# Hybrid decoder trunk with eight experts: three places of 96 slots, five lasting weight tiles, and five loads sent in halves

## The chip, the cores and the metric

The kernel runs on one core of a Trainium2 chip; the other seven cores do nothing. The metric is the device time of one execution in microseconds (us), here the median of three runs. The times of single instructions come from one further execution, which the hardware profiler recorded.

## The reference, cut to what matters

256 tokens of 1024 features pass through two layers and a last norm. Layer 0 (two kinds of attention, then a dense SwiGLU) and the attention of layer 1 are not touched by the change. What counts is the last block of layer 1, in which each token goes to the two experts with the highest router logits:

```python
def swiglu(x, w_gate, w_up, w_down):
    return (jax.nn.silu(x @ w_gate) * (x @ w_up)) @ w_down

def moe_swiglu(x, w_router, w_gate, w_up, w_down):      # x: 256 tokens x 1024
    logits = (xt @ w_router).astype(jnp.float32)        # 8 experts
    top_vals, top_idx = lax.top_k(logits, TOP_K)        # TOP_K = 2, ties to the lower index
    top_w = jax.nn.softmax(top_vals, axis=-1)
    gates = jnp.einsum('nk,nke->ne', top_w, jax.nn.one_hot(top_idx, N_EXPERTS, ...))
    for e in range(N_EXPERTS):                          # w_gate[e], w_up[e]: 1024 x 3584, w_down[e]: 3584 x 1024, float32
        y = y + gates[:, e:e + 1] * swiglu(xt, w_gate[e], w_up[e], w_down[e])
```

The 512 choices (256 tokens, two each) are all that has to be computed; the weights of all eight experts have to be read once, whoever uses them.

## The kernel before, in words

**Places and slots.** The experts are run in eight places, one after the other. Place 0 is always expert 0. Which of the experts 1 to 7 stands in places 1 to 7 is settled at run time: `choose` (L929) counts the tokens of each expert on VectorE (DVE), `arrange` (L959) ranks experts 1 to 7 by their count, and place i takes the expert whose rank is `RANKS[i-1]`. Place i has `CAPS[i]` slots, 64 or 96, and every matmul of the place is laid out for that many rows, filled or not. Where an expert has more tokens than its place has slots, `t.over` is positive and the branch at L1317 runs the surplus in a further pass (`rest`), which reads that expert's weights a second time.

**Loads.** The weights of one expert come in 12 loads of 3,584 KB: four of `w_gate`, four of `w_up`, four of `w_down`. That is 96 loads, numbered 1 to 96 here in the order in which they are sent. They go through five buffers in turn (buffer of load n is reused by load n+5), on the DMA queue of the sync engine (SP), which issues in program order: an issue that has to wait holds up all behind it. Loads 1 and 2 are brought in small pieces during layer 0 (`weights.piece`). `experts_open` (L1020) sends loads 3, 4 and 5 into the pool `big2`, which takes memory that layer 1 has just used. From then on `weights.send()` stands behind the matmuls that read a load: when load n has been read, load n+5 is sent into its buffer. The last load of `w_down`, load 96, is sent as three smaller ones.

**The matmuls of a place.** `into` (L1140) multiplies the gathered tokens with a gate or up load into PSUM, in two halves r of the 3,584 columns; `down` (L1186) does it with a `w_down` load. A place of 64 needs two groups of 32 rows, a place of 96 three, and the third group costs its own matmuls: 12 instead of 8 for each row block of a load in `into`, and in `down` those to `yo` (L1197). The order within a place is: two gate loads, two `w_down` loads of the place before, two up loads, two gate loads, two `w_down` loads of this place, two up loads. Between them stand the transposes of the hidden values (L1177), the gathers of the next group of places (L1101) and the scatter of the last place into the residual stream (L1224, L1225). TensorE (PE) runs this order as written.

**Before the experts.** The last projection of layer 1 (`w_out1`) is worked in four parts v0, v1, v2, v3 of 24 matmuls each, in that order, and each part reads one pair of split weight tiles (`whi`, `wlo`), which lie in the memory of three pools `parts0` to `parts2`. Router transposes and logits stand between the matmuls of v3 and behind them.

Of the kernel before, what the change touches and what calls it, by code (L numbers as in the profile page):

```python
# [31 lines left out]

CAPS = (64, 96, 64, 96, 96, 64, 96, 64)
RANKS = (0, 4, 1, 2, 5, 3, 6)

# [54 lines left out]
def trunk(ctx: ExitStack, tc: tile.TileContext, a: dict, out: bass.AP):  # L90
# [41 lines left out]

    turn = [0]

    def raw():
        n = sum(c for _, c, _ in raw_pools)
        i = turn[0] % n
        turn[0] += 1
        for pool, c, size in raw_pools:
            if i < c:  # L140
                break
            i -= c
        return pool.tile([128, size], F32, name="big")

# [172 lines left out]
    onesb = consts.tile([128, 128], BF, name="onesb")  # L317
    lower = consts.tile([128, NE, NE], F32, name="lower")
    place = consts.tile([128, 2, NE], F32, name="place")
    wr = consts.tile([128, KD, NE], F32, name="wr")  # L320
# [24 lines left out]
    def masks():  # L345
        V.tensor_scalar(tri, jp, 0.0, None, op0=OP.is_ge)
        V.tensor_scalar(mcaus[:, 0:128], jp[:, :128], 0.0, NEG, op0=OP.is_gt, op1=OP.mult)
        V.memset(mcaus[:, 128:256], 0.0)
        V.tensor_copy(mcaus[:, 256:384], mcaus[:, 0:128])
        V.tensor_copy(mswa[:, 0:128], mcaus[:, 0:128])  # L350
        V.tensor_scalar(mswa[:, 128:256], jp[:, :128], 0.0, NEG, op0=OP.is_le, op1=OP.mult)
        V.tensor_copy(mswa[:, 256:384], mcaus[:, 0:128])
        G.iota(slot, pattern=[[1, 128]], base=0, channel_multiplier=0, allow_small_or_imprecise_dtypes=True)
        V.tensor_scalar(strict, jp[:, :128], 0.0, None, op0=OP.is_gt)
        V.memset(onesb, 1.0)
        own, other = slot[:, 0:NE, None], slot[:, None, 0:NE]
# [570 lines left out]


    def choose():  # L929
        rp = t.rp  # L930
        t.lg = rp.tile([128, NB, NE], F32, name="lg")
        V.tensor_copy(t.lg, t.pl)
        gt = rp.tile([128, NB, NE, NE], BF, name="gt")
        eq = rp.tile([128, NB, NE, NE], BF, name="eq")
        t.rank = rp.tile([128, NB, NE], F32, name="rank")
        mb = rp.tile([128, NB, NE], BF, name="mb")
        other = t.lg[:, :, None, :].to_broadcast([128, NB, NE, NE])
        own = t.lg[:, :, :, None].to_broadcast([128, NB, NE, NE])
        V.tensor_tensor(eq, other, own, op=OP.is_equal)
        V.tensor_tensor(gt, other, own, op=OP.is_gt)  # L940
        V.tensor_tensor(eq, eq, lower[:, None, :, :].to_broadcast([128, NB, NE, NE]), op=OP.mult)
        V.tensor_tensor(gt, gt, eq, op=OP.add)
        V.tensor_reduce(t.rank, gt, axis=AX.X, op=OP.add)
        V.tensor_scalar(mb, t.rank, 2.0, None, op0=OP.is_lt)
        pp = bank(32)
        T.matmul(pp[:, 0:8], strict, mb[:, 0], start=True, stop=True)
        T.matmul(pp[:, 8:16], onesb, mb[:, 0], start=True, stop=False)
# [3 lines left out]
        far = rp.tile([128, NB, NE], F32, name="far")  # L951
        V.tensor_scalar(far, mb, -1000.0, 1000.0, op0=OP.mult, op1=OP.add)
        t.pos = rp.tile([128, NB, NE], F32, name="pos")
        V.tensor_tensor(t.pos, far, pp[:, 0:16].rearrange("p (b e) -> p b e", b=NB), op=OP.add)
        t.count = rp.tile([128, NE], F32, name="count")
        V.tensor_copy(t.count, pp[:, 16:24])


    def arrange():  # L959
        rp, n = t.rp, NE - 1  # L960
        sq = [128, n, n]
        c = t.count[:, 1:]
        more, same = rp.tile(sq, F32, name="more"), rp.tile(sq, F32, name="same")
        own, other = c[:, :, None].to_broadcast(sq), c[:, None, :].to_broadcast(sq)
# [3 lines left out]
        V.tensor_tensor(more, more, same, op=OP.add)  # L968
        rk = rp.tile([128, n], F32, name="rk")
        V.tensor_reduce(rk, more, axis=AX.X, op=OP.add)  # L970
        t.at = rp.tile(sq, F32, name="at")
        V.tensor_tensor(t.at, rk[:, None, :].to_broadcast(sq), place[:, 1, 1:, None].to_broadcast(sq), op=OP.is_equal)
# [11 lines left out]
    def moved(o, x):  # L984
        n = NE - 1
        p = t.rp.tile([128, n, n], F32, name="moved", bufs=2)
        V.tensor_tensor(p, t.at, x[:, None, 1:].to_broadcast([128, n, n]), op=OP.mult)
# [9 lines left out]
    def gates():  # L997
        rp = t.rp
        t.gate = gate = rp.tile([128, NB, NE], F32, name="gate")
        tw = rp.tile([128, 4, NB], F32, name="tw")  # L1000
        oh = [rp.tile([128, NB, NE], F32, name=f"oh{i}") for i in range(2)]
        mx = [rp.tile([128, NB], F32, name=f"mx{i}") for i in range(2)]
        for i in range(2):
# [9 lines left out]
        V.tensor_tensor(tw[:, 3], tw[:, 1], tw[:, 2], op=OP.mult)  # L1013
        gt2 = rp.tile([128, NB, NE], F32, name="gt2")
        V.tensor_tensor(gate, oh[0], bc(tw[:, 2]), op=OP.mult)
# [4 lines left out]
    def experts_open():  # L1020
# [7 lines left out]
        t.yo = py.tile([128, 256], F32, name="yo")  # L1028
        raw_pools.append((lpool("big2", 3), 3, BIG))
        turn[0] = 2  # L1030
# [23 lines left out]
    class Weights:  # L1054
# [29 lines left out]
    def experts(base, caps, groups, first=(), then=(), finish=()):  # L1084
# [45 lines left out]
        def part_out(e, g, j0, n):  # L1130
            def start(v):
                nc.sync.dma_start(v[:, :n * D], weight("down", e)[g * RG:(g + 1) * RG]
                                  .rearrange("(p j) w -> p (j w)", j=7)[:, j0 * D:(j0 + n) * D])
            return weights.add(start)
# [5 lines left out]
        def into(e, u, k0, key):  # L1140
# [155 lines left out]
    def final3(b):  # L1296
# [4 lines left out]
    finish = [do(final_in)] + [do(final2, b) for b in range(NB)] + [do(final3, b) for b in range(NB)]  # L1301
    mine = experts((0,) * NE, CAPS, ((0,), (1, 2), (3,), (4, 5), (6, 7)), [do(experts_open)],
                   [do(order.close), do(in_order, 'PE'), do(arrange), do(gates), do(read_counts)], finish)
# [52 lines left out]
```

## Time and profile before

| | us |
|---|---|
| median of three runs | 1336.55 (1336.16 to 1337.74) |
| the profiled execution, its own time | 1339.13 |
| its span, first to last instruction | 1337.3 |
| PE busy | 1285.7 (96%) |
| DVE busy | 373.7 (28%) |
| weights and other bytes moved by SP's queue | 428.48 MB, 80.0% of 16 engines' span |

The part with the experts begins near 504 us, when PE reads load 1, and takes the rest of the span. The busy share of PE counts every moment in which a matmul is somewhere in the array, so 96% doesn't yet say that PE decides the time. The other number to keep in view is the rate at which the DMA engines bring weights, stretch by stretch, and how long a load takes from its issue to its landing.

### The profile page before, as it was taken

The numbers are of one execution on the slowest core, as the hardware profiler recorded it, in microseconds if no ns is written. First come the engines' busy times: TensorE is split into PE (matmuls) and PEld (weight loads), VectorE is DVE, ScalarE is ACT, GpSimd is POOL, SyncE is SP. The second block draws the span as 40 slices with busy tenths as digits, with TensorE's granted clock in tenths as the row PEclk, the third lists the DMA queues.
The fourth block names the chain that finished last, engine by engine and source line by source line (L and its number), as shares of the span: only waits on it lengthen the run. The fifth ranks groups of instructions, "written<-read, shape, count | busy, mean of one in ns | idle before, by whom it ended". The sixth has DMA issues, their size and how long they took to land.

```text
span 1337.3 us, 23873 instructions
## 1 busy us (share of the span) xinstructions
PE 1285.7 (96%) x10713; PEld 697.2 (52%) x10713; DVE 373.7 (28%) x697; ACT 303.3 (23%) x495; POOL 167.3 (13%) x116
## 2 busy tenths in 40 slices
PE   7999899999999999999999898999999999999995
PEld 6876678888879783433333332433333343333332
DVE  7666445445465831001012001000201200100202
ACT  6565444443344621100000100100000010000001
POOL 3311344334434110000000000000000000000000
PEclk9999899999999999999999999999999999999997
DMA  8620785555555249999999999999999999999993
GB/s 272 207 93 1 294 287 189 182 177 178 187 166 181 95 183 433 415 427 431 422 426 430 416 428 425 424 432 386 397 384 399 429 420 428 434 419 426 427 426 134
DMA packets 75758, 431.71 MB, mean 323 GB/s; under 512 B 3676, under 2 KB 7792, under 8 KB 71424
## 3 DMA queue, kind: packets, MB, share of 16 engines
q1 hardware_dynamic: 75088, 428.48, 80.0%
q8 instruction: 86, 1.41, 0.4%
q0 software_dynamic: 416, 1.10, 0.2%
q10 hardware_dynamic: 144, 0.52, 0.1%
q14 instruction: 24, 0.20, 0.0%
HBM read 429.04 MB, written 1.05 MB: 322 GB/s over the span
## 4 chain that ended last, share of the span: by engine, by line
PE 82%; DMA 11%; DVE 2%; ACT 1%; POOL 1%; issue 0%; POOLq 0%; ACTq 0%
PE mm L1150 32%; PE y L1193 11%; PE mm L201 8%; PE mm L202 8%; PE mm L203 8%; DMA big<-in_l_w_up_dram 8%; PE yo L1197 4%; DMA big<-in_l_w_down_dram 2%; PE tt L1177 1%; PE tt L1101 1%; PE ww L373 1%; PE ww L203 1%; PE ww L201 1%; PE ww L202 1%; PE mm L416 1%; DMA raw<-in_l_w_gate_dram 1%
## 5 line engine op out<-in xcount | busy, mean ns | idle before, releaser
L1150 PE MATMUL mm<-big,g 128*32 128x448 f32 x5120 | 495.1, 544 | 11.6 <-DMA big<-in_l_w_up_dram 10.5
L1150 PEld LDWEIGHTS mm<-big,g 128*32 128x32 f32 x5120 | 165.4, 111 | 320.1 <-issue 297.5
L1193 PE MATMUL y<-big,ehT 128*32 128x512 f32 x1792 | 215.2, 593 | 0.4 <-DMA big<-in_l_w_down_dram 0.4
L164 POOL TENSOR_TENSOR wlo<-raw,whi 128x288 fp32r<-128x288 f32 (+6 forms) x74 | 154.5, 2089 | 287.2 <-ACT whi L160 266.5
L162 DVE TENSOR_TENSOR wlo<-raw,whi 128x1760 fp32r<-128x1760 f32 (+6 forms) x74 | 143.0, 1934 | 134.0 <-ACT whi L160 133.7
L160 ACT ACTIVATE whi<-raw 128x2048 fp32r<-128x2048 f32 (+4 forms) x74 | 134.4, 1816 | 154.2 <-PE mm L203 82.3
L201 PE MATMUL mm<-whi,xh 128*128 128x512 f32 (+3 forms) x352 | 139.1, 396 | 1.7 <-ACT whi L160 0.9
L202 PE MATMUL mm<-wlo,xh 128*128 128x512 f32 (+3 forms) x352 | 137.2, 390 | 3.0 <-POOL wlo L164 3.0
L203 PE MATMUL mm<-whi,xl 128*128 128x512 f32 (+3 forms) x352 | 137.0, 390 | 1.4 <-DVE xl L290 1.3
L1178 ACT ACTIVATE ehT<-tt 128x512 f32<-128x512 f32 (+1 forms) x32 | 15.6, 487 | 520.3 <-PE tt L1177 520.2
L1164 DVE TENSOR_TENSOR hid<-hid,mm 128x448 f32<-128x448 f32 x40 | 24.9, 621 | 306.8 <-PE mm L1150 303.7
L1294 POOL TENSOR_TENSOR fs<-fs,nhalf 128x1 f32<-128x1 f32 x2 | 1.1, 548 | 830.3 <-DVE fs L1293 830.3
L1193 PEld LDWEIGHTS y<-big,ehT 128*32 128x32 f32 x1792 | 56.9, 110 | 81.5 <-issue 62.9
L201 PEld LDWEIGHTS mm<-whi,xh 128*128 128x128 f32 x352 | 67.7, 192 | 17.6 <-issue 1.8
L202 PEld LDWEIGHTS mm<-wlo,xh 128*128 128x128 f32 x352 | 67.7, 192 | 16.9 <-POOL wlo L164 3.3
L203 PEld LDWEIGHTS mm<-whi,xl 128*128 128x128 f32 x352 | 67.3, 191 | 16.8 <-DVE xl L290 3.1
L1197 PE MATMUL yo<-big,ehT 128*32 128x256 f32 x896 | 68.9, 379 | 0.0
L1197 PEld LDWEIGHTS yo<-big,ehT 128*32 128x32 f32 x896 | 29.1, 110 | 67.0 <-issue 65.3
L201 PE MATMUL mm<-xh,whi 128*128 128x256 f32 x160 | 46.6, 291 | 0.0
L202 PE MATMUL mm<-xl,whi 128*128 128x256 f32 x160 | 45.2, 283 | 0.0
L203 PE MATMUL mm<-xh,wlo 128*128 128x256 f32 x160 | 45.2, 283 | 0.0
L1180 DVE COPY ehT<-tt 128x384 f32<-128x384 f32 x16 | 8.9, 558 | 124.0 <-PE tt L1177 124.0
(310 smaller groups left out, 1048.0 us busy)
## 6 DMA issues: line engine op xcount, KB each, us to landing
big<-in_l_w_up_dram SPq DMA_DIRECT2D x32, 3584.0 KB, 26.8
big<-in_l_w_down_dram SPq DMA_DIRECT2D x31, 3584.0 KB, 26.2
big<-in_l_w_gate_dram SPq DMA_DIRECT2D x30, 3584.0 KB, 24.7
raw<-in_l_w_in_dram SPq DMA_DIRECT2D x15, 1024.0 KB, 5.0
raw<-in_l_w_gate_dram SPq DMA_DIRECT2D x14, 1024.0 KB, 5.0
raw<-in_l_w_up_dram SPq DMA_DIRECT2D x14, 1024.0 KB, 5.0
raw<-in_l_w_down_dram SPq DMA_DIRECT2D x14, 1024.0 KB, 4.9
raw<-in_l_w_out_dram SPq DMA_DIRECT2D x8, 1024.0 KB, 5.0
```

The costliest lines, as they stand in the source:

```text
L160: A.activation(hi, v, AF.Copy)
L162: V.tensor_tensor(lo[:, :, :m], v[:, :, :m], hi[:, :, :m].bitcast(F32), op=OP.subtract)
L164: G.tensor_tensor(lo[:, :, m:], v[:, :, m:], hi[:, :, m:].bitcast(F32), op=OP.subtract)
L201: T.matmul(ps, l[0], r[0], start=first, stop=False, **kw)
L202: T.matmul(ps, l[0], r[1], start=False, stop=False, **kw)
L203: T.matmul(ps, l[1], r[0], start=False, stop=last, **kw)
L373: T.matmul(p[:, i, Q], q[i][:, qs], k[i][:, 0:n], start=True, stop=bias is None)
L1150: T.matmul(ps[key][j][i * O:(i + 1) * O], x[:, k0 + k, g * O:(g + 1) * O], w[:, k, c:c + CH], **at)
L1164: V.tensor_tensor(x[:, g], x[:, g], ps["u"][g], op=OP.mult)
L1178: copy = V.tensor_copy if j0 else lambda a_, b_: A.activation(a_, b_, AF.Copy)
L1193: T.matmul(t.y[c * O:(c + 1) * O], x[:, (2 * i + c % 2) * O:(2 * i + c % 2 + 1) * O], w[:, j, c // 2 * 512:(c // 2 + 1) * 512], **at)
L1197: T.matmul(t.yo[c * O:(c + 1) * O], x[:, (4 + i) * O:(5 + i) * O], w[:, j, c * 256:(c + 1) * 256], **at)
```

## The change

It has five parts. Place 4 goes from 96 slots to 64, so three places of 96 are left (1, 3 and 5) with places of 64 between them; ranks and groups of places are rearranged to fit. The five buffers become five tiles that are allocated once and kept (`buffers`), so that a load waits for the readers of the part that it overwrites and not for the release of a whole tile; `big2` becomes three pools of one tile. Loads 6 to 10 are sent in two parts: the first (`half`) behind the readers of the first half of its buffer, the second where the whole load went before. The many small tiles of the router move from their own pool `rp` into the first 600 or so columns of a tile that is free by then (`tmp` in `t.dr[0]`). And `choose` ranks the logits with three DVE operations (subtract, compare with `least`, sum) instead of five.

```diff
-CAPS = (64, 96, 64, 96, 96, 64, 96, 64)
-RANKS = (0, 4, 1, 2, 5, 3, 6)
+CAPS = (64, 96, 64, 96, 64, 96, 64, 64)
+RANKS = (0, 3, 1, 4, 2, 5, 6)
...
-    turn = [0]
+    turn, buffers = [0], {}
     def raw():
...
-        return pool.tile([128, size], F32, name="big")
+        if at not in buffers:
+            buffers[at] = pool.tile([128, size], F32, name="big")
+        return buffers[at]
...
+        V.tensor_scalar(least, lower, -2.0 ** -126, None, op0=OP.mult)
...
+    def tmp(*shape):
+        n = math.prod(shape)
+        v = t.dr[0][:, t.used:t.used + n]
+        t.used += n
...
-        V.tensor_tensor(eq, other, own, op=OP.is_equal)
-        V.tensor_tensor(gt, other, own, op=OP.is_gt)
-        V.tensor_tensor(eq, eq, lower[:, None, :, :].to_broadcast([128, NB, NE, NE]), op=OP.mult)
-        V.tensor_tensor(gt, gt, eq, op=OP.add)
+        V.tensor_tensor(gt, other, own, op=OP.subtract)
+        V.tensor_tensor(gt, gt, least[:, None, :, :].to_broadcast([128, NB, NE, NE]), op=OP.is_gt)
         V.tensor_reduce(t.rank, gt, axis=AX.X, op=OP.add)
...
-        raw_pools.append((lpool("big2", 3), 3, BIG))
+        raw_pools.extend((lpool(f"big{i}"), 1, BIG) for i in range(2, 5))
...
         def send(self):
             if self.at < len(self.todo):
                 x = self.todo[self.at]
                 self.at += 1
+                if x.tile is not None:
+                    x.start(x.tile, 2, 2)
+                    return
                 x.tile = raw()
                 x.start(x.tile)
+        def half(self):
+            if len(self.todo) > 90 and 5 <= self.at < 10:
+                x = self.todo[self.at]
+                x.tile = raw()
+                x.start(x.tile, 0, 2)
...
         def part_out(e, g, j0, n):
-            def start(v):
-                nc.sync.dma_start(v[:, :n * D], weight("down", e)[g * RG:(g + 1) * RG]
-                                  .rearrange("(p j) w -> p (j w)", j=7)[:, j0 * D:(j0 + n) * D])
+            def start(v, i=0, m=4):
+                a, b = (0, 3, n)[i // 2], (0, 3, n)[(i + m) // 2]
+                nc.sync.dma_start(v[:, a * D:b * D], weight("down", e)[g * RG:(g + 1) * RG]
+                                  .rearrange("(p j) w -> p (j w)", j=7)[:, (j0 + a) * D:(j0 + b) * D])
...
         def into(e, u, k0, key):
...
+                if k == 1:
+                    weights.half()
             weights.send()
...
-    mine = experts((0,) * NE, CAPS, ((0,), (1, 2), (3,), (4, 5), (6, 7)), [do(experts_open)],
+    mine = experts((0,) * NE, CAPS, ((0,), (1, 2), (3, 4), (5, 6), (7,)), [do(experts_open)],
```

Instructions move in two places. The first is SP's queue where the expert loads begin. Before, the third to tenth load (the rows with `big`) stand there so, each with the engines or queues that it waits for; `most` is the table of places that SP reads:

```order
93 L1124 DMA big<-in_l_w_up_dram 128x4x1792 [waits DVE_49,DMASW1_49,PE_49,Activation_49]
94 L1124 DMA big<-in_l_w_up_dram 128x4x1792 [waits DVE_49,PE_49,Pool_49]
95 L1124 DMA big<-in_l_w_gate_dram 128x4x1792
96 L1036 TENSOR_LOAD most [waits DVE_49]
97 L1036 ISA x2
98 L1124 DMA big<-in_l_w_gate_dram 128x4x1792 [waits PE_49]
99 L1132 DMA big<-in_l_w_down_dram 128x7168 [waits PE_49]
100 L1132 DMA big<-in_l_w_down_dram 128x7168 [waits DMAHW4_49,PE_49]
101 L1124 DMA big<-in_l_w_up_dram 128x4x1792 [waits DMAHW5_49,DMAHW2_49,PE_49]
102 L1124 DMA big<-in_l_w_up_dram 128x4x1792 [waits DMAHW6_49,DMAHW3_49,PE_49]
```

In the changed kernel the same stretch of SP's queue reads:

```order
93 L1147 DMA big<-in_l_w_up_dram 128x4x1792 [waits DVE_49,DMASW1_49,PE_49,Activation_49]
94 L1147 DMA big<-in_l_w_up_dram 128x4x1792 [waits PE_49]
95 L1147 DMA big<-in_l_w_gate_dram 128x4x1792 [waits PE_49,Pool_49]
96 L1049 TENSOR_LOAD most [waits DVE_49]
97 L1049 ISA x2
98 L1147 DMA big<-in_l_w_gate_dram 128x2x1792 [waits PE_49] x2
99 L1156 DMA big<-in_l_w_down_dram 128x3072 [waits PE_49]
100 L1156 DMA big<-in_l_w_down_dram 128x4096 [waits DMAHW2_49,PE_49]
101 L1156 DMA big<-in_l_w_down_dram 128x3072 [waits DMAHW4_49,DMAHW3_49,PE_49]
102 L1156 DMA big<-in_l_w_down_dram 128x4096 [waits PE_49]
```

Loads 6 to 10 (row 98 and after) have become two issues each. The waits of loads 4 and 5 (rows 94 and 95) have changed with the memory under them. Before, `rp` ends at byte 111,712 of each partition, the three tiles of `big2` reach up to byte 197,728, and load 4 has the topmost, whose last 1,152 bytes lie in `parts0` (from byte 196,576), where the split weights of v3 are. In the built program load 4 waits for the last matmul of v3, and load 5 stands behind it in the queue and waits for nothing more. In the changed kernel `rp` ends at byte 109,664 and the three tiles end at byte 195,680, below `parts0`. Load 4 now lies over the weights of v1 (in `parts2`) and waits for the last matmul of v1; load 5 lies over those of v2 (in `parts1`) and waits for the last matmul of v2 and for v2's split on POOL.

The second place is PE's order at the change from place 3 to place 4, in r=0 of place 4. Before, both have 96 slots (`mm` is the PSUM tile of gate and up, `hid` the hidden values, `g` the gathered tokens):

```order
2343 L1150 MATMUL mm<-big,g 32x448 x96
2344 L1224 MATMUL tt<-raw,dispT 128x512
2345 L1225 MATMUL tt<-raw,dispT 128x512
...
2352 L1150 MATMUL mm<-big,g 32x448 x48
2353 L1177 MATMUL tt<-ident,hid 128x128 x7
2354 L1150 MATMUL mm<-big,g 32x448 x48
2355 L1177 MATMUL tt<-ident,hid 64x128 x7
```

In the changed kernel place 4 has 64 slots:

```order
2338 L1174 MATMUL mm<-big,g 32x448 x64
2339 L1250 MATMUL tt<-raw,dispT 128x512
2340 L1251 MATMUL tt<-raw,dispT 128x512
...
2347 L1174 MATMUL mm<-big,g 32x448 x32
2348 L1203 MATMUL tt<-ident,hid 128x128 x7
2349 L1174 MATMUL mm<-big,g 32x448 x32
2350 L1124 MATMUL tt<-disp,xg 128x160 x8
```

Each load of place 4 is read by 32 matmuls instead of 48, the second transpose is gone, and the gather of places 5 and 6 stands here.

## Rows read from the trace of the kernel before

**Rows 1.** The page, parts 1 and 2: PE busy, and GB/s in 40 slices.

```profile
PE 1285.7 (96%) x10713; PEld 697.2 (52%) x10713; DVE 373.7 (28%) x697; ACT 303.3 (23%) x495; POOL 167.3 (13%) x116
...
GB/s 272 207 93 1 294 287 189 182 177 178 187 166 181 95 183 433 415 427 431 422 426 430 416 428 425 424 432 386 397 384 399 429 420 428 434 419 426 427 426 134
```

**Rows 2.** The page, part 4: the chain that ended last, by engine.

```profile
PE 82%; DMA 11%; DVE 2%; ACT 1%; POOL 1%; issue 0%; POOLq 0%; ACTq 0%
```

**Rows 3.** Busy time by stretch; last columns: granted clock, DMA share, GB/s.

```profile
530.00:870.00 340.00, 329.86 (x3311) 123.78 (x3307) 32.32 (x62) 28.84 (x66) 0.00 (x0) 0.99 1.01 425
940.00:1050.00 110.00, 109.10 (x1186) 41.43 (x1182) 12.21 (x26) 7.34 (x16) 0.00 (x0) 1.00 0.97 394
```

**Rows 4.** SP's timeline: first issue, time to the end of the last, count.

```profile
469.39 24.78 SPq L1124 DMA_DIRECT2D big<-in_l_w_up_dram  x2
494.22 16.56 SPq L1124 DMA_DIRECT2D big<-in_l_w_gate_dram  x2
...
833.07 12.43 SPq L1124 DMA_DIRECT2D big<-in_l_w_up_dram  x2
...
898.42 9.40 SPq L1124 DMA_DIRECT2D big<-in_l_w_up_dram  x2
...
1015.17 6.40 SPq L1124 DMA_DIRECT2D big<-in_l_w_up_dram  x2
...
1076.73 8.89 SPq L1124 DMA_DIRECT2D big<-in_l_w_gate_dram  x2
...
1106.12 9.40 SPq L1124 DMA_DIRECT2D big<-in_l_w_up_dram  x2
...
1278.11 19.40 SPq L1132 DMA_DIRECT2D big<-in_l_w_down_dram  x4
```

**Rows 5.** DMA issues one by one (loads 3, 6, 27, 46, 71, 95); last: us to landing.

```profile
big<-in_l_w_up_dram SPq DMA_DIRECT2D x1, 3584.0 KB, 12.2
...
big<-in_l_w_gate_dram SPq DMA_DIRECT2D x1, 3584.0 KB, 14.6
...
big<-in_l_w_up_dram SPq DMA_DIRECT2D x1, 3584.0 KB, 27.0
...
big<-in_l_w_up_dram SPq DMA_DIRECT2D x1, 3584.0 KB, 28.1
...
big<-in_l_w_gate_dram SPq DMA_DIRECT2D x1, 3584.0 KB, 22.2
...
big<-in_l_w_down_dram SPq DMA_DIRECT2D x1, 3584.0 KB, 29.9
```

**Rows 6.** DMA issues between 940 and 1050 us; median us to landing.

```profile
big<-in_l_w_up_dram SPq DMA_DIRECT2D x4, 3584.0 KB, 13.8
```

**Rows 7.** SP's waits between 466 and 512 us: total, times, longest.

```profile
SPq L1124 <- PE mm L203: 24.0, 1, 24.0
```

**Rows 8.** PE's timeline from the output projection to the first load: start, us.

```profile
467.69 0.80 PE L201 MATMUL mm<-whi,xh 128*128 128x512 f32 x1
...
479.38 0.39 PE L203 MATMUL mm<-whi,xl 128*128 128x512 f32 x1
...
484.82 0.39 PE L203 MATMUL mm<-whi,xl 128*128 128x512 f32 x1
...
500.13 3.80 PE L1101 MATMUL tt<-disp,xg 128*128 128x64 f32 x32
504.13 6.22 PE L1150 MATMUL mm<-big,g 128*32 128x448 f32 x64 [0.20 <-issue]
```

**Rows 9.** Timelines of DVE and ACT between the logits and the gather.

```profile
497.57 0.28 DVE L941 TENSOR_TENSOR eq<-eq,lower 128x128 bf16<-128x128 bf16 x1
...
498.79 1.15 ACT L907 ACTIVATE xg<-h,rs 128x1024 f32<-128x1024 f32 x1 [2.38 <-POOL rs L906]
```

**Rows 10.** Busy time by stretch, columns as in rows 3, around a wait.

```profile
757.00:769.00 12.00, 8.16 (x84) 3.02 (x80) 0.00 (x0) 0.57 (x2) 0.00 (x0) 1.00 1.02 420
769.00:777.00 8.00, 7.84 (x64) 2.31 (x64) 0.64 (x2) 0.00 (x0) 0.00 (x0) 0.79 1.01 421
```

More of the change, by code (lines that the diff above doesn't have):

```diff
@@ L138, in raw @@
         turn[0] += 1
+        at = i
         for pool, c, size in raw_pools:
@@ L318, in trunk @@
     lower = consts.tile([128, NE, NE], F32, name="lower")
+    least = consts.tile([128, NE, NE], F32, name="least")
     place = consts.tile([128, 2, NE], F32, name="place")
@@ L926, in bc @@
         return v[:, :, None].to_broadcast([128, NB, NE])
+    def tmp(*shape):
+        n = math.prod(shape)
+        v = t.dr[0][:, t.used:t.used + n]
+        t.used += n
+        if len(shape) == 1:
+            return v
+        names = "abc"[:len(shape)]
+        return v.rearrange(f"p ({' '.join(names)}) -> p {' '.join(names)}", **dict(zip(names, shape)))
     def choose():
         rp = t.rp
-        t.lg = rp.tile([128, NB, NE], F32, name="lg")
+        t.used = 0
+        t.lg = tmp(NB, NE)
         V.tensor_copy(t.lg, t.pl)
-        gt = rp.tile([128, NB, NE, NE], BF, name="gt")
-        eq = rp.tile([128, NB, NE, NE], BF, name="eq")
-        t.rank = rp.tile([128, NB, NE], F32, name="rank")
+        gt = tmp(NB * NE, NE).rearrange("p (b e) f -> p b e f", b=NB)
+        t.rank = tmp(NB, NE)
         mb = rp.tile([128, NB, NE], BF, name="mb")
@@ L950, in choose @@
         T.matmul(pp[:, 16:24], onesb, mb[:, 1], start=False, stop=True)
-        far = rp.tile([128, NB, NE], F32, name="far")
+        far = tmp(NB, NE)
         V.tensor_scalar(far, mb, -1000.0, 1000.0, op0=OP.mult, op1=OP.add)
-        t.pos = rp.tile([128, NB, NE], F32, name="pos")
+        t.pos = tmp(NB, NE)
         V.tensor_tensor(t.pos, far, pp[:, 0:16].rearrange("p (b e) -> p b e", b=NB), op=OP.add)
-        t.count = rp.tile([128, NE], F32, name="count")
+        t.count = tmp(NE)
         V.tensor_copy(t.count, pp[:, 16:24])
@@ L962, in arrange @@
         c = t.count[:, 1:]
-        more, same = rp.tile(sq, F32, name="more"), rp.tile(sq, F32, name="same")
+        more, same = tmp(n, n), tmp(n, n)
         own, other = c[:, :, None].to_broadcast(sq), c[:, None, :].to_broadcast(sq)
@@ L968, in arrange @@
         V.tensor_tensor(more, more, same, op=OP.add)
-        rk = rp.tile([128, n], F32, name="rk")
+        rk = tmp(n)
         V.tensor_reduce(rk, more, axis=AX.X, op=OP.add)
-        t.at = rp.tile(sq, F32, name="at")
+        t.at = tmp(n, n)
+        t.moved = [tmp(n, n) for _ in range(2)]
         V.tensor_tensor(t.at, rk[:, None, :].to_broadcast(sq), place[:, 1, 1:, None].to_broadcast(sq), op=OP.is_equal)
@@ L985, in moved @@
         n = NE - 1
-        p = t.rp.tile([128, n, n], F32, name="moved", bufs=2)
+        p = t.moved[0]
+        t.moved.reverse()
         V.tensor_tensor(p, t.at, x[:, None, 1:].to_broadcast([128, n, n]), op=OP.mult)
@@ L998, in gates @@
         rp = t.rp
[L999 to L1002, printed above, removed]
+        gate, tw = tmp(NB, NE), tmp(4, NB)
+        oh, mx = [tmp(NB, NE) for _ in range(2)], [tmp(NB) for _ in range(2)]
         for i in range(2):
@@ L1013, in gates @@
         V.tensor_tensor(tw[:, 3], tw[:, 1], tw[:, 2], op=OP.mult)
-        gt2 = rp.tile([128, NB, NE], F32, name="gt2")
+        gt2 = tmp(NB, NE)
         V.tensor_tensor(gate, oh[0], bc(tw[:, 2]), op=OP.mult)
```

## The prediction

> **What bounds the kernel now.** First the page. PE is busy 96% of the span [rows 1] and holds 82% of the chain that ended last, the DMA engines 11% [rows 2]. Read alone, this says that TensorE is the bound and that fewer matmuls are time saved. The GB/s line beneath says something else: from the 16th slice (each 33.4 us) the core moves some 425 GB/s almost without pause, and the only sag is in slices 28 to 31 (386, 397, 384, 399). By stretch it is the same: 425 GB/s at a DMA share of 1.01 from 530 to 870 us, 394 at 0.97 from 940 to 1050 [rows 3]. Two bounds alternate: mostly the load stream, around 900 to 1050 PE.
>
> I make this sharp by landings. Load 6 is issued at 494.22 + 16.56 - 0.38 (one issue) = 510.40 and lands 14.6 later, at 525.0. Load 46 is issued at 833.07 + 12.43 - 0.38 = 845.12 and lands at 873.2, load 71 at 1076.73 + 22.2 = 1098.9, load 95 at 1278.11 + 29.9 = 1308.0 [rows 4, 5]. So 40 loads took 348.2 us (8.705 each), the next 25 took 225.7 (9.03 each), the last 24 took 209.1 (8.71 each). 8.71 us is the stream's own pace; the middle 25 lost 25 x (9.03 - 8.71) = 8.0 us. The reason is in the time from issue to landing. A load issued to an empty queue (load 3) lands after 12.2 us; load 27 needed 27.0, since it stood behind others [rows 5]; between 940 and 1050 the median is 13.8 [rows 6]. There the queue has run dry when a load is issued: PE frees the buffers too late. PE needs 1015.17 - 898.42 = 116.75 us for the 12 loads that it reads in place 4 (loads 47 to 58, whose buffers go to loads 52 to 63, so the issues of 51 and 63 bound them), the stream 12 x 8.71 = 104.5; in place 5, with 64 slots, PE takes 1106.12 - 1015.17 = 90.95 [rows 4]. One wide place costs the stream nothing, the five buffers absorb it. Places 3 and 4 in a row are too much.
>
> The second loss is where the stream begins. Load 3 goes out at 469.39, load 4 only at 493.80, after a wait of 24.0 us in all for the L203 matmuls of the output projection [rows 4, 7].
>
> **The change part by part.**
>
> *Place 4 with 64 slots.* From one issue to the next (subtracting 0.38 for the issue in the row) a load of a wide place holds its buffer 9.40 - 0.38 = 9.02 us, of a narrow one 6.40 - 0.38 = 6.02 [rows 4], so PE loses about 12 x 3.0 = 36 us of work. Not all of it becomes time, since the stream needs 8.71 a load whatever PE does. What is won is the starvation, 8.0 us, if it goes wholly. A wide place then follows a narrow one: 116.75 less 2 x 3.0 (its first two `w_down` loads now belong to a narrow place) is 110.7, or 6 us behind the stream; the narrow place behind it, about 91 to 93 with the wider gather, takes back 12 to 13. Load 27, issued at the end of place 1, now waits 27.0 us to land. With a stream that runs some 5.5 us earlier (below) that is 21.5, later wide places come no closer, and dryness begins at 12.2. So the stream doesn't run dry. Bounds: 4 us if half of it stays; 10.5 if all four slices rise to 425 (133.7 us x (1 - 391.5/425)) [rows 1]. I take 8.0, the count of landings.
>
> *The memory under loads 4 and 5.* Load 4 now waits for the last of v1, the 48th matmul from 467.69: it starts at 479.38, so the load goes at about 479.8 instead of 493.8. Load 5 waits for the 72nd, 484.82, and goes at about 485.2 instead of 494.2 [rows 8]. Nothing else stands in SP's queue there. With load 3 landing at 481.6, loads 4 and 5 follow at 8.71 each, until about 499.
>
> *Halves.* Load 6 waits for PE to read load 1, which starts at 504.13 and takes 6.2 [rows 8]; the first half is free after 3.1, so it goes at 507.2 instead of 510.4. But the queue is now empty, from about 499. A load into an empty queue takes 12.2 [rows 5], so load 6 lands at 507.2 + 12.2 = 519.4 (its second half goes at 510.4, while the first is still moving) instead of 525.0: 5.5 us won. Without the halves it would be 510.4 + 12.2 = 522.6, 2.4 won. At best the start-up is hidden, 507.2 + 8.7 = 515.9, 9.1 won. Then PE frees a half every 3.1 us and the stream takes 4.35 for one, so it doesn't run dry again; loads 7 to 10 gain nothing more of their own, and their five extra issues of 0.38 us lie in SP's waits.
>
> The Trainium skill (DMA: Bandwidth & Descriptors, Specifications) puts the fabric ceiling at 435 GB/s. By that a load of 3.67 MB would take an estimated 8.44 us, the 89 from load 6 to load 95 would take 751 instead of 775, and the gain would be about 37 us. The trace's pace of 8.71 over 64 loads decides here.
>
> *Router.* Two of five dependent DVE operations of 0.28 us go [rows 9], some 0.4 us of chain. The gather starts at 500.13 [rows 8], just behind ACT's `xg` copy, which ends at 498.79 + 1.15 = 499.94 [rows 9] and doesn't depend on them: 0. If that cover were gone, 0.4 would be won. Lasting tiles and scratch in `t.dr[0]` add no operation: 0.
>
> *Sum.* Last landing 1308.0 - 5.5 - 8.0 = 1294.5. Behind load 95 stand 1337.3 - 1308.0 = 29.3 us (two `w_down` loads read, scatter, last norm), unchanged, since place 7 has 64 slots in both and PE waits for its loads at the end. Span 1323.8, own time 1339.13 - 13.5 = 1325.6. The profiled run was 2.6 above the median, so the median becomes 1336.55 - 13.5 = 1323.0.
>
> **Rivals.**
>
> *PE is the bound, as the page's shares say.* All 36 us come off: 1300.5. Against it: at 8.71 a load the 89 loads alone take 775 us, and the stream already runs at a share of 1.01 for 340 us [rows 3]. 2%.
>
> *The early start is lost*, because PE or SP comes later than I think to load 6: only the 8.0 stay, 1328.5. 9%. *The starvation stays*, because the narrow places don't give back enough: only the 5.5 stay, 1331.0. 6%. For the second speaks PE's 97% from 530 to 870 [rows 3]; against it the 21.5 us worked out above. 2% for both being lost, 1336.5.
>
> *The stream is quicker than its landings.* Counted in bytes, the sag costs 10.5, and with 9.1 at the start the gain is 19.6: 1317.0. 10%.
>
> *PE's clock falls in the new waits.* With less to do, PE waits some 2.5 us for each load once it has caught up. In the trace, 757 to 769 has 3.84 us of idle PE, and in the stretch behind it the granted clock is 0.79, part of it at 1.2 GHz instead of 2.4; its 64 matmuls fill 7.84 us instead of 6.2 [rows 8, 10]. That is 1.6 per drop. PE has such slack everywhere except in the last two loads: 1324.6. The Trainium skill (TensorE: Matmul & The Clock Gate, Part 1) says that a PE waiting for DMA between bursts falls back to half rate; the trace agrees for this wait, with 0.79. 4%.
>
> *Slower: an expert overflows.* Place 4 now takes the fourth of experts 1 to 7 and has 64 slots. The reference's own router, run on its inputs, gives them 72, 69, 65, 64, 62, 61 and 61 tokens, and expert 0 has 58. So three exceed 64 and the fourth fills its place exactly. With 65 the branch at the end would run: 12 more loads at 8.71 are 104.5 us or more, 1427.5. One token chosen differently decides it; the smallest gap between a second and a third logit is 0.005. 3%.
>
> **How the numbers follow.** The sum as it stands has 64%, and with the rivals that is 100. The predicted time is its time, 1323.0. The range is 1317.0 to 1329.5: it takes in the quicker stream, the clock and the lost early start, which leaves 13% outside. It is also about what the bounds make: at best 9.1 + 10.5, at worst 2.4 + 4. A measurement here can tell 0.2%, 2.7 us, from no change. All cases but two are faster by more than that: 95%; no change 2%; slower 3%.
>
> **What would show each step.** Loads 4 and 5 issued near 480 and 485; a hole in the stream from about 499 to 508; the first part of load 6 issued near 507 and the whole landed near 519.5. No stretch of low GB/s between 900 and 1050, and issue to landing there well above 13.8. Load 95 near 1294.5 and 29 us behind it. PE's waits for weight DMAs grow by some 22 us (36 less 13.5). The prediction is wrong if load 6 lands no earlier than 522, if the landings of loads 46 to 71 are still more than 8.8 us apart, or if the pace elsewhere leaves 8.71.

## The result, and the profile after

The changed kernel takes 1324.87 us (median of four runs, 1322.55 to 1326.17); beside it the kernel before took 1337.14 (four runs, 1336.16 to 1340.99). The ratio is 0.9893, 95% interval 0.9868 to 0.9918, some 14.3 us less by the ratio (11.0 to 17.6); the two medians lie 12.3 apart. The prediction said 1323.0, in a range from 1317.0 to 1329.5. The profiled execution took 1322.55, its span is 1320.8.

The page of the changed kernel: PE busy, GB/s in 40 slices, and the chain that ended last, by engine.

```profile
PE 1250.8 (95%) x10219; PEld 676.4 (51%) x10219; DVE 368.6 (28%) x686; ACT 300.2 (23%) x489; POOL 167.3 (13%) x116
...
GB/s 276 208 96 1 284 297 174 185 191 180 177 163 185 126 319 325 421 427 432 422 426 427 419 428 424 425 431 421 427 429 417 427 428 423 430 426 425 426 423 104
...
PE 75%; DMA 17%; DVE 2%; ACT 1%; POOL 1%; issue 0%; POOLq 0%; ACTq 0%; DVEq 0%
```

Beside [rows 1, 2]: PE lost 34.9 us of work, twice what the span lost. The sag in slices 28 to 31 is gone; nothing from slice 17 to 39 is under 417. Slice 15 has risen from 183 to 319, since loads 4 and 5 go earlier; slice 16 has fallen from 433 to 325, and in it lies a new hole at the start. The DMA share of the chain rose from 11% to 17%.

Busy time by stretch in the changed kernel (columns as in rows 3):

```profile
530.00:870.00 340.00, 335.21 (x3408) 125.38 (x3404) 32.40 (x62) 27.28 (x62) 0.00 (x0) 0.99 1.01 425
940.00:1050.00 110.00, 104.39 (x1004) 37.41 (x996) 9.44 (x17) 8.36 (x20) 0.00 (x0) 0.98 1.01 424
```

Between 940 and 1050 the stream now moves 424 GB/s, where it moved 394 [rows 3]; PE is idle there 5.6 us instead of 0.9. The DMA issues of the same 110 us (last column: median us from issue to landing):

```profile
big<-in_l_w_gate_dram SPq DMA_DIRECT2D x4, 3584.0 KB, 33.7
big<-in_l_w_down_dram SPq DMA_DIRECT2D x4, 3584.0 KB, 35.4
big<-in_l_w_up_dram SPq DMA_DIRECT2D x4, 3584.0 KB, 33.4
```

Where the median was 13.8 [rows 6], a load now lands 33 to 35 us after its issue, so the stream no longer runs dry there. SP's timeline gives the start and the end (first issue, time to the end of the last, count):

```profile
467.48 9.88 SPq L1147 DMA_DIRECT2D big<-in_l_w_up_dram  x2
482.47 24.84 SPq L1147 DMA_DIRECT2D big<-in_l_w_gate_dram  x3
...
823.25 12.43 SPq L1147 DMA_DIRECT2D big<-in_l_w_up_dram  x2
...
1053.06 10.45 SPq L1147 DMA_DIRECT2D big<-in_l_w_gate_dram  x2
...
1254.98 23.07 SPq L1156 DMA_DIRECT2D big<-in_l_w_down_dram  x4
```

and single issues their landing: the two halves of load 6, then loads 46, 71 and 95.

```profile
big<-in_l_w_gate_dram SPq DMA_DIRECT2D x1, 1792.0 KB, 8.3
...
big<-in_l_w_gate_dram SPq DMA_DIRECT2D x1, 1792.0 KB, 9.6
...
big<-in_l_w_up_dram SPq DMA_DIRECT2D x1, 3584.0 KB, 29.3
...
big<-in_l_w_gate_dram SPq DMA_DIRECT2D x1, 3584.0 KB, 29.4
...
big<-in_l_w_down_dram SPq DMA_DIRECT2D x1, 3584.0 KB, 36.6
```

Load 4 goes at 467.48 + 9.88 - 0.37 = 476.99 and load 5 at 482.47, where they went at 493.80 and 494.22 [rows 4]. The last issue of the three is load 6's second half: 482.47 + 24.84 - 0.37 = 506.94, and with 9.6 it lands at 516.5. Load 46 lands at 835.3 + 29.3 = 864.6, load 71 at 1082.5, load 95 at 1291.6. So 40 loads took 8.70 us each, the next 25 8.72, the last 24 8.71.

Times from the start of the execution mix the change with what happens before it, so one more row is needed, PE's timeline where the experts begin:

```profile
496.57 0.41 PE L1124 MATMUL tt<-disp,xg 128*128 128x64 f32 x2
497.17 3.56 PE L1124 MATMUL tt<-disp,xg 128*128 128x64 f32 x30 [0.19 <-ACT xg L912]
500.67 6.22 PE L1174 MATMUL mm<-big,g 128*32 128x448 f32 x64
```

The trace has two records for each matmul of float32 operands, so x64 stands for the 32 matmuls that read load 1. PE's first matmul on load 1 stands at 500.67, before at 504.13 [rows 8]. Counted from there, load 6 lands after 15.8 us instead of 20.9, and load 95 after 1291.6 - 500.7 = 790.9 instead of 1308.0 - 504.1 = 803.9. That is 12.9 us, the part of the change in the load stream: 5.0 at the start and 7.9 from there to load 95, 7.7 of them between loads 46 and 71. Of the 16.5 by which the spans differ, another 3.5 lie ahead of load 1: 0.6 between the first router matmul and load 1, 2.8 ahead of the router, where the experiments will show scatter of that size and more.

### The profile page after: what moved, and what is told of

It reads as the page before. It is cut to its first block, busy times and chain, and to the rows that moved or that the text cites. A ratio compares the mean times of both kernels' runs of the same rounds, so it can differ in the third digit from the quotient of the medians.

```text
span 1320.8 us, 22875 instructions
## 1 busy us (share of the span) xinstructions
PE 1250.8 (95%) x10219; PEld 676.4 (51%) x10219; DVE 368.6 (28%) x686; ACT 300.2 (23%) x489; POOL 167.3 (13%) x116
## 4 chain that ended last, share of the span: by engine, by line
PE 75%; DMA 17%; DVE 2%; ACT 1%; POOL 1%; issue 0%; POOLq 0%; ACTq 0%; DVEq 0%
PE mm L1174 29%; DMA big<-in_l_w_up_dram 13%; PE y L1219 9%; PE mm L204 8%; PE mm L205 8%; PE mm L206 8%; PE yo L1223 3%; DMA big<-in_l_w_gate_dram 3%; PE ww L378 1%; PE tt L1203 1%; PE tt L1124 1%; PE ww L206 1%; PE ww L204 1%; PE ww L205 1%; DMA raw<-in_l_w_gate_dram 1%; PE mm L421 1%
## 5 line engine op out<-in xcount | busy, mean ns | idle before, releaser
L1174 PE MATMUL mm<-big,g 128*32 128x448 f32 x4864 | 474.7, 548 | 21.6 <-DMA big<-in_l_w_up_dram 15.4
L1174 PEld LDWEIGHTS mm<-big,g 128*32 128x32 f32 x4864 | 156.8, 111 | 319.8 <-issue 287.1
L1223 PE MATMUL yo<-big,ehT 128*32 128x256 f32 x672 | 51.7, 379 | 0.0
L1223 PEld LDWEIGHTS yo<-big,ehT 128*32 128x32 f32 x672 | 21.8, 110 | 50.3 <-issue 49.0
```

Source lines behind the costliest of these rows:

```text
L1223: T.matmul(t.yo[c * O:(c + 1) * O], x[:, (4 + i) * O:(5 + i) * O], w[:, j, c * 256:(c + 1) * 256], **at)
```

## The experiments

In the table t1 is the start of PE's first matmul on load 1. "Load 6" and "load 95" are their landings counted from t1, the pace is the landing of load 71 less that of load 46, over 25, and the tail runs from the landing of load 95 to the end of the span. Each row is one profiled execution; the times are medians of the timed runs, and the ratio is to the kernel before beside it.

| kernel | us (runs) | ratio, 95% interval | t1 | load 6 | pace 46 to 71 | load 95 | tail |
|---|---|---|---|---|---|---|---|
| before | 1337.14 (4) | | 504.1 | 20.9 | 9.03 | 803.9 | 29.4 |
| changed | 1324.87 (4) | 0.9893 (0.9868 to 0.9918) | 500.7 | 15.8 | 8.72 | 790.9 | 29.2 |
| changed, again | 1325.71 (5) | 0.9906 (0.9889 to 0.9924) | 504.1 | 15.8 | 8.73 | 791.2 | 28.7 |
| places only | 1330.78 (6) | 0.9947 (0.9930 to 0.9964) | 502.1 | 21.3 | 8.72 | 796.5 | 30.2 |
| old places | 1333.10 (12) | 0.9965 (0.9946 to 0.9983) | 505.4 | 15.5 | 8.97 | 797.2 | 30.5 |
| no halves | 1329.03 (6) | 0.9931 (0.9913 to 0.9949) | 502.7 | 17.5 | 8.72 | 793.9 | 30.0 |
| late start | 1333.52 (12) | 0.9969 (0.9953 to 0.9985) | 504.6 | 21.2 | 8.72 | 796.5 | 30.2 |
| three in a row | 1346.54 (4) | 1.0073 (1.0058 to 1.0089) | 500.7 | 15.9 | 8.92 | 814.1 | 29.7 |
| five operations, first | 1333.24 (1) | | 511.6 | 15.8 | 8.72 | 791.1 | 28.8 |
| five operations, timed | 1326.62 (5) | 0.9917 (0.9903 to 0.9930) | 504.7 | 15.9 | 8.72 | 791.4 | 29.0 |
| quarters and tail | 1325.45 (4) | 0.9911 (0.9896 to 0.9926) | 504.3 | 15.4 | 8.72 | 792.0 | 28.4 |

**Places only.** The kernel before with the three tables of the change and nothing else.

```diff
-CAPS = (64, 96, 64, 96, 96, 64, 96, 64)
-RANKS = (0, 4, 1, 2, 5, 3, 6)
+CAPS = (64, 96, 64, 96, 64, 96, 64, 64)
+RANKS = (0, 3, 1, 4, 2, 5, 6)
...
-    mine = experts((0,) * NE, CAPS, ((0,), (1, 2), (3,), (4, 5), (6, 7)), [do(experts_open)],
+    mine = experts((0,) * NE, CAPS, ((0,), (1, 2), (3, 4), (5, 6), (7,)), [do(experts_open)],
```

> The kernel before with the new slots, ranks and groups of places alone. Theory A (the gain is two separate losses of the load stream, 8 us of starvation in places 3 and 4 and 5 us at its start): only the starvation goes, so 8 us less than before, some 1329 us; the 25 loads from 46 to 71 land 8.71 us apart instead of 9.03, and load 6 lands 20.9 us after PE begins to read load 1, as before. Theory B (the time follows PE's work): this kernel has all of the saved matmuls, so nearly the whole gain, 13 to 14 us, some 1323 us.

7.1 us were won in the timing, and load 95 came 7.3 earlier. The start is that of before: SP's timeline has load 5 at 492.56 and load 6 at 492.56 + 16.17 - 0.37 = 508.36, and load 6 lands 21.3 us after t1.

```profile
468.65 23.85 SPq L1124 DMA_DIRECT2D big<-in_l_w_up_dram  x2
492.56 16.17 SPq L1124 DMA_DIRECT2D big<-in_l_w_gate_dram  x2
```

The pace between loads 46 and 71 is 8.72 and the stretch from 940 to 1050 shows 425 GB/s (columns as in rows 3):

```profile
940.00:1050.00 110.00, 103.04 (x988) 37.15 (x984) 9.43 (x17) 8.36 (x20) 0.00 (x0) 0.98 1.01 425
```

So the narrow place alone ends the starvation, and that is all that it is worth. Its page shows PE 31.8 us less busy than before:

```profile
PE 1253.9 (94%) x10219; PEld 678.2 (51%) x10219; DVE 369.0 (28%) x687; ACT 300.0 (23%) x489; POOL 167.3 (13%) x116
```

That PE is the bound, at 36 us for the removed matmuls, is ruled out.

**Old places.** The changed kernel with the old tables: the rest of the change without place 4.

```diff
-CAPS = (64, 96, 64, 96, 64, 96, 64, 64)
-RANKS = (0, 3, 1, 4, 2, 5, 6)
+CAPS = (64, 96, 64, 96, 96, 64, 96, 64)
+RANKS = (0, 4, 1, 2, 5, 3, 6)
...
-    mine = experts((0,) * NE, CAPS, ((0,), (1, 2), (3, 4), (5, 6), (7,)), [do(experts_open)],
+    mine = experts((0,) * NE, CAPS, ((0,), (1, 2), (3,), (4, 5), (6, 7)), [do(experts_open)],
```

> The changed kernel with the old slots, ranks and groups: lasting tiles, loads 4 and 5 over the early-freed memory, halves and the short router stay. Theory A: load 6 lands 15.8 us after PE begins load 1 instead of 20.9, the stream runs dry in places 3 and 4 as before, 5 to 5.5 us less than before, some 1332 us. Theory B: PE has the old work, so no gain beyond the router's 0.6 us, 1336 us. Theory C (an earlier stream only runs into the wide places earlier, and gives its lead back there): also about 1336, but with load 6 early and the landings of loads 46 to 71 further apart than 9.03 us.

4.7 us by the timing. Load 6 lands 15.5 after t1, so the whole gain at the start is there, 5.3 us; the starvation is back, with 398 GB/s from 940 to 1050:

```profile
940.00:1050.00 110.00, 109.09 (x1186) 41.47 (x1182) 12.90 (x26) 7.80 (x16) 0.00 (x0) 1.00 0.98 398
```

It is a little milder, 25 x (8.97 - 8.71) = 6.5 us instead of 8.0. By load 95 the two parts won 7.3 and 6.7, together 14.0 where the change has 12.9: about 1 us is counted in both, since the earlier stream by itself softens the starvation.

**No halves.** The changed kernel without the early first part: loads 6 to 10 go whole, where load 1 to 5 have been read.

```diff
-                if k == 1:
-                    weights.half()
```

> The changed kernel without the halves: loads 6 to 10 go whole, behind all readers of their buffer. Theory A: load 6 is issued 3.1 us later into a queue that is empty by then, so it lands 18.6 to 19 us after PE begins load 1 instead of 15.8, and the whole kernel is 3 us slower than the changed one, 10.5 to 11 us less than before. Rival D (the loads queue up again at once, so the halves only move waits): no difference to the changed kernel, 13.5 us or more less than before.

Against the changed kernel (1324.87, and 1325.71 in the repeat) 3.3 to 4.2 us are lost; load 95 comes 2.9 later. At load 6 only 1.7 of these show (17.5 instead of 15.8), less than expected. Load 6 is issued whole at 484.10 + 25.22 - 0.37 = 508.95 by SP's timeline, and lands 11.2 later, not 12.2:

```profile
484.10 25.22 SPq L1147 DMA_DIRECT2D big<-in_l_w_gate_dram  x2
```

```profile
big<-in_l_w_gate_dram SPq DMA_DIRECT2D x1, 3584.0 KB, 11.2
```

The rest comes just behind it. From load 6 to load 7 it takes 9.7 us here and 8.5 and 8.8 in the two executions of the changed kernel; from there to load 95 they are equal to 0.1 us. So the halves are worth nearly the 3 us that the prediction gave them (2.9, and 2.7 against the repeat), some 1 us of them in load 7, whose first part is also early. What the early loads 4 and 5 win without the halves is the difference to places only at load 95, 796.5 - 793.9 = 2.6 us.

**Late start.** The changed kernel with a 2,048-byte tile that nothing uses in `rp` and with the old pool of three, which puts loads 4 and 5 where they lay before. The halves stay.

```diff
+        t.rp.tile([128, 512], F32, name="space")
...
-        raw_pools.extend((lpool(f"big{i}"), 1, BIG) for i in range(2, 5))
+        raw_pools.append((lpool("big2", 3), 3, BIG))
```

> The changed kernel with an unused 2,048-byte tile in the router's pool and the old pool of three tiles, so that the buffers of loads 4 and 5 lie where they lay before and both loads wait for the last matmul of the output projection; the halves stay. Theory A: the queue then never runs empty before load 6, so the halves have nothing to win, load 6 lands 20.9 us after PE begins load 1, and 5 us of the gain go: 8 to 8.5 us less than before, some 1329 us. Rival E (the halves are worth their 3 us on their own, wherever the loads before them stand): 11 us less than before.

SP's timeline has load 5 at 494.94, as before the change, and load 6 lands at 21.2: the gain at the start is gone (20.9 before the change), though load 6's first half still goes at t1 + 3.3.

```profile
470.05 24.84 SPq L1148 DMA_DIRECT2D big<-in_l_w_up_dram  x2
494.94 16.29 SPq L1148 DMA_DIRECT2D big<-in_l_w_gate_dram  x3
```

The halves need the empty queue that the early loads 4 and 5 leave; alone they win nothing, and neither do the lasting tiles, which are in this kernel too: load 95 came 7.4 us earlier than before, what the places alone give (7.3). The timing shows less, 4.1 us (2.0 to 6.3) where 8 to 8.5 were expected, with twelve runs from 1329.3 to 1338.8. The trace puts 0.5 us of the difference in t1 and 0.9 in the tail; the other 2 are not explained.

**Three in a row.** The changed kernel with its three wide places moved together: 1, 2 and 3.

```diff
-CAPS = (64, 96, 64, 96, 64, 96, 64, 64)
-RANKS = (0, 3, 1, 4, 2, 5, 6)
+CAPS = (64, 96, 96, 96, 64, 64, 64, 64)
+RANKS = (0, 1, 2, 3, 4, 5, 6)
```

> The changed kernel with its three places of 96 in a row (places 1, 2 and 3) instead of 1, 3 and 5. The matmuls are the same in number and shape but for one gather (columns 160, 128, 64 after the second place instead of 160, 160, 64). Theory A (five buffers absorb one wide place, not several in a row): load 27 still lands some 21 us after its issue, place 2 falls 15 to 17 us behind the stream, place 3 another 12, and below 12.2 us of lead the stream runs dry: loads 30 to 50 land about 10 us apart, some 15 to 20 us more than the changed kernel, 1340 to 1345 us, slower than before. Theory B (the time follows PE's work): within 2 us of the changed kernel.

Matmuls, bytes and instructions are those of the changed kernel (PE x10219 in both), and it is 21 us slower than that (1324.87 and 1325.71), and 0.7% slower than before. Its page and its stretch from 760 to 960 us (columns as in rows 3), with the issues in it:

```profile
PE 1254.8 (93%) x10219; PEld 677.4 (50%) x10219; DVE 368.8 (27%) x686; ACT 300.3 (22%) x489; POOL 167.5 (12%) x116
```

```profile
760.00:960.00 200.00, 198.57 (x2165) 76.77 (x2167) 20.16 (x42) 15.24 (x35) 0.00 (x0) 1.00 0.95 380
```

```profile
big<-in_l_w_down_dram SPq DMA_DIRECT2D x8, 3584.0 KB, 12.9
big<-in_l_w_gate_dram SPq DMA_DIRECT2D x7, 3584.0 KB, 11.6
big<-in_l_w_up_dram SPq DMA_DIRECT2D x6, 3584.0 KB, 13.0
```

PE is busy 198.6 of 200 us, the loads land 11.6 to 13.0 us after their issue and the stream makes 380 GB/s. Load 95 is 23.2 us later than in the changed kernel. Loads 30 to 50 land 9.9 us apart, about as expected; the time came out a little above the 1340 to 1345 us expected. It is the neighbourhood of the wide places that costs, not the sum of their matmuls.

**Five operations.** The changed kernel with the ranking of before, first a single run, then timed.

```diff
-        V.tensor_tensor(gt, other, own, op=OP.subtract)
-        V.tensor_tensor(gt, gt, least[:, None, :, :].to_broadcast([128, NB, NE, NE]), op=OP.is_gt)
+        eq = tmp(NB * NE, NE).rearrange("p (b e) f -> p b e f", b=NB)
+        V.tensor_tensor(eq, other, own, op=OP.is_equal)
+        V.tensor_tensor(gt, other, own, op=OP.is_gt)
+        V.tensor_tensor(eq, eq, lower[:, None, :, :].to_broadcast([128, NB, NE, NE]), op=OP.mult)
+        V.tensor_tensor(gt, gt, eq, op=OP.add)
```

> The changed kernel with the five operations of the old ranking in choose, on the same scratch. From the first router matmul to the first matmul on load 1 the trace of before shows 15.01 us and that of the changed kernel 14.37. If the two operations are worth it: 14.9 to 15.1 here. If they are hidden behind the copy of xg: 14.4 to 14.7, and the stage differs between executions only by PE's clock. The rest as in the changed kernel.

The single run gave 1333.24, far off. Its trace says where: t1 is 511.6 instead of 500.7, while load 95 stands 791.1 us behind t1, as in the changed kernel. 7.8 us of the delay are there by 175 us, in layer 0, which no version touches. The stretch from 60 to 120 us, first with five operations, then in the changed kernel:

```profile
60.00:120.00 60.00, 58.68 (x337) 44.70 (x335) 37.48 (x93) 34.21 (x84) 10.39 (x7) 0.91 0.27 88
```

```profile
60.00:120.00 60.00, 58.72 (x360) 43.92 (x359) 39.34 (x102) 35.71 (x94) 8.98 (x6) 1.00 0.25 82
```

PE's granted clock is 0.91 there instead of 1.00, and it got through 337 matmuls instead of 360. A single time is no reading of a 0.4 us edit, so the kernel was timed:

> The same edit as the single run with five ranking operations, now timed in rounds. Theory A: the three operations are hidden by ACT's copy of xg, and the 10 us that the single run lay above the changed kernel came from its half-clock stretches ahead of the experts: the median is within 1.5 us of the changed kernel's 1324.9 to 1325.7, and from PE's first matmul on load 1 to the landing of load 95 it takes 790.9 to 791.4 us. Rival: the two operations saved are what matters, and the time stays near 1333.

1326.62, within 0.9 to 1.8 us of the two medians of the changed kernel, and load 95 lands 791.4 behind t1: the rival, at 1333, is out. A little remains ahead of t1. From the first router matmul to t1 the four executions with five operations took 14.6 to 15.1 us (15.01 in the kernel before, 14.61, 15.05, 15.10), the seven others 14.4 to 14.7, a mean difference of 0.3 us. By this stage the expectation of the single run came out on its other side, 14.9 to 15.1: the saved operations are not wholly hidden, though the two groups overlap and 0.3 is less than either scatters.

**Quarters and tail.** The changed kernel with load 6 in three parts (a quarter, a quarter, a half) and load 95 in two (four and three rows).

```diff
-                if k == 1:
-                    weights.half()
+                if k < 2:
+                    weights.half(k)
...
+                if self.at == 5:
+                    if k == 0:
+                        x.tile = raw()
+                    x.start(x.tile, k, 1)
...
-            return steps_out(e, 2 * r) + steps_out(e, 2 * r + 1, sizes)
+            return steps_out(e, 2 * r, (4, 3) if len(sizes) > 1 else (7,)) + steps_out(e, 2 * r + 1, sizes)
```

> The changed kernel with two steps more in the same direction: load 6 goes in a quarter, a quarter and a half, the first quarter behind the first of load 1's four row blocks, and load 95 goes as two loads of four and three row blocks, so that PE can begin on it earlier. Theory A: the first part of load 6 is issued 1.5 us earlier into an empty queue, so load 6 lands 14.2 to 14.5 us after PE begins load 1 instead of 15.8; and at the end PE no longer reads the whole of load 95 after it has landed, so the 29.2 us from there to the end become 26 to 27. Together 4 to 4.5 us less than the changed kernel, some 1320.5 us. Rival F: the queue's start-up takes the same however early a small first part goes (no gain at load 6), and the end is held by the last landing and what follows it, not by PE's reading (no gain there).

1325.45, no better; neither of the two expected gains came. The first part goes 1.5 us earlier (t1 + 1.8), but load 6 lands only 0.4 earlier: its last half still waits until load 1 is read, at t1 + 6.3, and takes 9.1 from there. By load 95 even that is gone (792.0). In the tail the split has nothing to remove. PE's timeline at the reading of the last two loads, in the changed kernel and in its repeat:

```profile
1291.75 12.22 PE L1219 MATMUL y<-big,ehT 128*32 128x512 f32 x112 [0.32 <-ACT ehT L1204]
...
1295.39 12.22 PE L1219 MATMUL y<-big,ehT 128*32 128x512 f32 x112 [0.43 <-DMA big<-in_l_w_down_dram]
```

and with load 95 in two parts:

```profile
1296.27 12.22 PE L1224 MATMUL y<-big,ehT 128*32 128x512 f32 x112 [0.32 <-ACT ehT L1209]
```

PE waits 0.43 us for load 95 in the repeat. In the first execution it waits 0.32 for ACT's copy of the hidden values instead, and with load 95 in two parts it does the same. The 112 matmuls then run without a gap, 12.22 us in all three. What follows is scatter and norm.

**Changed, again.** The changed kernel once more, beside three in a row, the first run with five operations, and quarters and tail, for the repeatability of the table's columns.

> The changed kernel as it is, beside the kernel before on the chip of this call, for the comparison with the two experiments: 12 to 15 us less than before. Theory A expects in its trace the same spacing of landings (8.71 us) and the same 15.8 us from the first matmul on load 1 to the landing of load 6, and that what differs between executions lies ahead of the experts, where PE's granted clock dips at different moments.

t1 moved by 3.4 us between its two profiled executions, load 95 behind t1 by 0.2. The granted clock from 420 to 486 us was 1.00 in the first and 0.95 in this one, as in the kernel before.

## Why the prediction was right, point by point

*The bound.* Two bounds in turn, as read from the landings: places only, old places and three in a row each moved load 95 by what the stream lost or won, and the 31.8 us by which places only shortened PE's work bought 7.3.

*Place 4: 8.0 us.* Measured 7.9 by load 95 beside the early start, 7.3 without it. A wide place between narrow ones costs the stream nothing: load 27, for which 21.5 us from issue to landing was forecast, took 20.8, and no later one took less.

*Loads 4 and 5.* Forecast 479.8 and 485.2 for an output projection that ended as before; they went at 476.99 and 482.47, and in the repeat, whose t1 is that of before, at 480.0 and 485.5.

*The start: 5.5 us.* Measured 5.0 in the change, 5.3 in old places. The forecast let the whole load 6 land 12.2 us after its first half was issued (t1 + 15.3); it landed 12.6 after it (t1 + 15.8). Load 6's second half took 9.6 us from its own issue. The hole in the stream stands in the windows (columns as in rows 3):

```profile
499.00:508.00 9.00, 9.00 (x94) 4.07 (x97) 2.29 (x20) 2.26 (x8) 0.00 (x0) 1.00 0.34 108
508.00:520.00 12.00, 12.00 (x136) 4.14 (x132) 0.04 (x1) 2.03 (x3) 0.00 (x0) 1.00 1.02 427
```

The halves were given 3.1 of it, and 2.7 to 2.9 were measured, but not all in load 6: the whole load 6 takes 11.2 and not 12.2, the halved one 12.6, so the halves win only 1.7 there, and load 7, which was to gain nothing of its own, brings the rest. That these two errors nearly cancel is luck. Without the early loads 4 and 5 the halves are worth nothing, which the prediction didn't say.

*Router: 0.* Not quite. PE's first two gather matmuls wait for nothing here, and the third waits 0.19 for ACT's `xg` (timeline above): the cover is about as long as what it covers. Some 0.3 us may have come off, a size below what the timing tells.

*The tail: unchanged.* 29.4 before, 29.2 and 28.7 after. Over all executions it lies between 28.4 and 30.5, for which no cause was looked for.

*The sum.* 13.5 us were forecast; the stream gave 12.9 and the router perhaps 0.3. The medians came to 1324.87 and 1325.71, 12.3 and 11.9 below the runs beside them and 1.9 and 2.7 above the 1323.0 forecast. (The interval of the first ratio reaches from 11.0 to 17.6.) The profiled executions lie further apart, 16.5 in the span, but the 3.5 of it in t1 is as much as t1 moved between two executions of the changed kernel (3.4): that part is scatter, and no merit of the forecast.

*The clock as a rival.* The first median lies nearer to this rival's 1324.6 than to 1323.0, so it needs an answer. Behind some of its new waits PE does fall to half clock. PE's waits between 504 and 1300 us in the changed kernel (total, times, longest):

```profile
PE mm L1174 <- DMA big<-in_l_w_up_dram: 15.4, 9, 2.7
PE y L1219 <- DMA big<-in_l_w_down_dram: 7.4, 5, 2.4
...
PE mm L1174 <- DMA big<-in_l_w_gate_dram: 6.2, 5, 2.5
```

That is 29.0 us, where the kernel before waited 11.4 in the same stretch: 17.6 more, not the 22 forecast. PE's busy time from t1 to the landing of load 95, before and changed (columns as in rows 3), fell by 30.1 us and not by 36:

```profile
504.13:1307.98 803.85, 786.81 (x8064) 295.24 (x8064) 81.47 (x161) 64.78 (x143) 0.00 (x0) 0.99 1.00 420
500.67:1291.61 790.94, 756.75 (x7571) 278.93 (x7570) 76.44 (x146) 61.85 (x137) 0.00 (x0) 0.98 1.00 422
```

Slower matmuls behind such waits eat part of the slack. In these stretches the granted clock falls to 1.2 GHz three times before and seven times in the changed kernel, and the 64 matmuls of one load take 7.92 us behind such a wait instead of 6.22; by that, four more falls are an estimated 7 us.

```profile
1274.52 7.92 PE L1174 MATMUL mm<-big,g 128*32 128x448 f32 x64 [2.60 <-DMA big<-in_l_w_up_dram]
```

Two windows around that wait show that it costs nothing while a load is still on its way:

```profile
1265.00:1275.00 10.00, 6.88 (x64) 1.93 (x64) 0.00 (x0) 0.00 (x0) 0.00 (x0) 0.98 1.03 429
1275.00:1285.00 10.00, 9.16 (x84) 3.29 (x80) 0.00 (x0) 0.00 (x0) 0.00 (x0) 0.85 1.01 427
```

PE idles 3.1 us in the first, the granted clock is 0.85 in the second (part of it at 1.2 GHz instead of 2.4), and the stream moves 427 GB/s all the same. The Trainium skill (TensorE: Matmul & The Clock Gate, Part 1) describes a kernel whose PE waits for DMA between bursts and falls back to half rate each time; the trace agrees for this wait, but not for every one (19 waits for loads, seven falls). The rival's 1.6 us would have to stand in the last two loads, where PE has no slack: their 112 matmuls take 12.22 us (timeline above) and the tail is no longer than before, so the rival is out. The fabric ceiling of 435 GB/s that the Trainium skill gives (DMA: Bandwidth & Descriptors, Specifications) was not reached: 3.67 MB in 8.71 us are 421, in every stretch in which the queue was kept full.

*What stays open.* The median of late start (4.1 us) lies apart from its landing (7.4 us by load 95, less 0.9 in the tail); that of no halves fits (9.2 us by the ratio; 10.0 by load 95, less 0.6 in the tail). t1 differs by 5 us between executions of kernels that are nearly alike up to there (500.7 and 505.4), so the rest is no more than that scatter allows, but it wasn't pinned down.

## What to carry to other kernels

Where a stream of loads and an engine alternate as the bound, find the stretch in which issue to landing falls to its least: here only there did the engine's work buy time, and its order (heavy places apart, not together) mattered more than its sum. At a cold start, look at what memory the first loads are laid over: 1,152 bytes of overlap held load 4 back by some 13 us, counted from t1, of which 2.6 came through to load 95 alone and some 5 together with the halves. Compare versions from a mark in the trace at which the touched part begins; here it repeated to 0.4 us in four executions (two of the changed kernel, two with five operations), while whole times differed by up to 11 us for reasons ahead of it.

## What the runs showed of the hardware

- Half a load is not half the time: 1,792 KB into the empty queue took 8.3 us from issue to landing, the next 1,792 KB, issued 3.0 us later, 9.6; the whole 3,584 KB took 11.2 and, at load 3 of the kernel before, 12.2. Cutting finer (quarters) brought the first part forward by 1.5 us and the landing by 0.4.
- Programs that are nearly alike up to the router began the experts between 500.7 and 511.6 us. In the latest the granted clock was 0.91 from 60 to 120 us, in the earliest 1.00.
- How long a load stands between issue and landing tells who waits: at 33 to 35 us the stream made 424 GB/s and PE idled, at 14 to 15 us it made 394 to 398 (the kernel before and old places), at 12 to 13 us 380 (three in a row).
